# Plain products for the first 1024 columns of each MLP, and the seven products' activation sums made beside them

## The chip, the core and the metric

The kernel runs on one core of one Trainium2 chip. The metric is the device time of one execution in microseconds (us). TensorE (PE in the profile) multiplies; VectorE (DVE) and ScalarE (ACT) prepare its operands and clear its accumulators; SyncE (SP) issues the loads of the weights; GpSimd (POOL) issues the adding transfers of the residual stream.

## What is computed

Two decoder layers on 256 tokens of width 2048, each with an attention part and an MLP. The part that matters here is the MLP, twice:

```python
def sq_relu_mlp(h, w_up, w_down):
    u = jax.nn.relu(h @ w_up)
    return (u * u) @ w_down
...
        h = h + sq_relu_mlp(rmsnorm(h, mlp_norm[i]), w_up[i], w_down[i])
```

`w_up` is 2048 x 8192 and `w_down` 8192 x 2048, all in float32. The gain of the norm is put into the activations before the product, and the scale of each row of tokens, which comes out of the squared activations as its square, is applied when the output of `w_down` is added to the residual stream.

## The kernel before

**Numbers.** A float32 number is carried as a high part and a rest, both in the reduced form that TensorE takes (`fp32r`). `split` (L191 to L194) makes both: ACT copies to the high part (L193), DVE subtracts it from the source (L194). A product of two such numbers is three matmuls (`mm3`, L196 to L199: high with high, high with rest, rest with high). The three of a `gemm` stand in its line L410.

**Weights.** They arrive in tiles `wraw` of two chunks of 128 rows by 1024 columns (1 MB a load). Three such tiles lie in the pool `wp`. In an MLP (`more[0]` set) three more in the pool `mlp` are taken in turn with them, and two of those three first hold something else: `gx`, the activations of one half of the 2048 inputs, for as long as sums are still to be made from them. The split weights lie in `whi` (5 buffers in an MLP) and `wlo` (5), each 128 x 1024.

**An MLP.** The 8192 inner columns are taken in eight blocks of 1024 (`NE = 8`). `up(e)` makes block e of `h @ w_up`; `down(e - 1)` then multiplies the block before it with its rows of `w_down`, in two `gemm`s of 8 chunks by 12 matmuls. So the order is up 0, up 1, down 0, up 2, down 1, and so on. Between up 0 and up 1 stands nothing else.

**Seven products.** `up(e)` treats 12 of the 16 chunks of inputs in the way of Strassen (the Winograd form): for a pair of chunks, its partner four chunks on, two blocks of 128 tokens and two of 512 columns, seven products take the place of eight. `seven` is called three times a block, for chunks (0, 1), (8, 9) and (10, 11) with their partners. Each call has seven `product`s of 6 matmuls (L197 to L199), each with its own split of 128 x 1024 weights, and four differences of weights on DVE (L775, L777, L779, L782). The other four chunks (2, 3, 6, 7) are multiplied plainly by four calls of `plain`, 12 matmuls and one split each. Together that is 174 matmuls of 512 columns, 25 splits and 12 differences a block. The eight accumulators fill all of PSUM: six `acc` and the two `side` banks, which transposes use too.

**The activations for it.** `form_steps` transposes the residual stream on PE (L302), copies it with the gain to `gx` on ACT (L319) and splits seven forms of each half: a11, a12, a22 as they are, and s1, s2, s4, s3, which are sums made on DVE (L327). Those of half 0 are made beside the second `gemm` of `project` (the output projection of the attention part). Half 1 needs the columns that this `gemm` finishes: its transposes follow at once, and its seven forms (`late`) come within `up(0)`, where three plain calls stand first and `seven` of half 0 next.

**Order.** Every engine runs its own list in a fixed order. The lists are made by a scheduler that takes instructions in the order of the code, but lets one that is ready by its own reckoning pass one that is not; a load is issued when a tile of its pool comes free. So work that stands late in the code can run early, and the order of loads is not that of the code.

After `up(0)` its block is squared and transposed at once (`flush`), ahead of `up(1)`: L821 and L822 on ACT, L421 on PE, L423 on ACT, L424 on DVE. For the other blocks that runs beside a `down`.

Of the kernel before, what the change touches and what calls it, by code (L numbers as in the profile page):

```python
# [11 lines left out]
F32 = mybir.dt.float32  # L12
# [80 lines left out]
def yoco_kernel(ctx: ExitStack, tc: tile.TileContext, x, a_w_in, a_w_out, w_kv, b_w_q, b_w_out, w_up, w_down,  # L93
# [199 lines left out]
    def form_steps(halves, half, which):  # L293

        n, plain, f = halves[half]

# [27 lines left out]
        def sum_form(name, a, b, op):  # L324
# [4 lines left out]

        on_pe = [lambda c=c: split_plain(c) for c in range(2)] if plain is not None else []  # L330
        on_pe += [lambda c=c, c2=c2: take(c, c2) for c in range(2) for c2 in range(n // 2)]
        add, sub = ALU.add, ALU.subtract
        rest = [lambda: split_form("a11", a11), lambda: split_form("a12", a12),
                lambda: sum_form("s1", a21, a22, add), lambda: sum_form("s2", a11, "s1", sub),
                lambda: sum_form("s4", a12, "s2", add), lambda: sum_form("s3", a11, a21, sub),
                lambda: split_form("a22", a22)]
        return on_pe, rest

# [53 lines left out]
    def gemm(stat, ks, w, row0, cols, evac, width=HALF, before=None, first_raw=None, by_column=False):  # L392
# [287 lines left out]
    def project(oTs, w, gain_next, cut, again):  # L680


        st = Stats()
        stat = stat_of(oTs)
        cols = [(n * GW, n * GW + HALF) for n in range(2)]
        forms = []

        def heads_done(k=cut):
            if k == cut:
                flush()  # L690
                open_scope("mlp")
# [9 lines left out]
        on_pe, rest = form_steps(forms, 0, gain_next)  # L701
        enqueue([(run(on_pe + rest), len(on_pe + rest))], 8)
        gemm(stat, range(cut if again else 0, KC), w, 0, cols[1], residual(st, 1), by_column=True)
        flush()
        on_pe, rest = form_steps(forms, 1, gain_next)
        for step in on_pe:
            step()
        return st, forms, rest

    st, xm, late = project(oTs, a_w_out[0], G_M0, CUT_A, True)  # L710


    NE = DFF // GW

    def mlp(i, xm, late, st_in, gains_next, final=None):


        us = {}
        more[0] = True
        r2 = st_in.inv_square()  # L720

        def up(e):

            if e == 0:

                q5, q7, q2, q4, q3, q8 = (ps.tile([P, HALF], F32, name="acc") for _ in range(6))
                q1, q6 = side(), side()
            else:  # L730
                q1, q6, q5, q7, q3, q8 = (ps.tile([P, HALF], F32, name="acc") for _ in range(6))
                q2, q4 = side(), side()
            banks = dict(q1=q1, q2=q2, q3=q3, q4=q4, q5=q5, q6=q6, q7=q7, q8=q8)
# [54 lines left out]
            def nearly_done():  # L788
                if e:
                    plain(1, 0)  # L790
                nc.scalar.copy(c11, q1)
# [3 lines left out]

            if e == 0:
                plain_rows()
                plain(0, 0)
                plain(0, 1)
                plain(1, 0)  # L800
# [5 lines left out]
            else:  # L806
# [6 lines left out]
            for c, q in ((c21, q4), (c12, q3), (c22, q8)):  # L813
                nc.vector.tensor_tensor(c, q, c, op=add)
            tiles = [new_xt() for _ in range(2)]
            us[2 * e], us[2 * e + 1] = tiles

            def transposes():
                yield
                for n, t, c in ((0, 0, c11), (0, 1, c21), (1, 0, c12), (1, 1, c22)):  # L820
                    nc.scalar.activation(c, c, AF.Relu)  # L821
                    nc.scalar.activation(c, c, AF.Square)  # L822
# [3 lines left out]

            enqueue([(transposes(), 6)], 6)
            if e == 0:
                flush()

        st = Stats()
# [13 lines left out]
        for e in range(NE):  # L845
            up(e)
            if e:
# [6 lines left out]

    st, (xkv, xq) = mlp(0, xm, late, st, [G_KV, G_B])
    open_scope("keep", "att")
# [81 lines left out]

    st, xm, late = project(oTs, b_w_out[0], G_M1, CUT_B, False)

# [80 lines left out]

    mlp(1, xm, late, st, [], final)
    scope[0].close()
# [34 lines left out]
```

## Time and profile before

| | |
|---|---|
| three runs | 2211.4, 2213.1 and 2213.3 us, median 2213.1 |
| the profiled execution | 2211.9 us, of which its span (first to last instruction) 2210.0 us |
| granted TensorE clock | 0.995 of full, mean of the span |
| DVE split `wlo` (L194), 128 x 1024 | 1.22 us, one every 1.14 us in a row |
| ACT high part `whi` (L193), 128 x 1024 | 1.05 us |
| DVE difference of weights (L775 and so on) | 1.22 us, one every 1.14 us in a row |
| load of 1 MB of `w_up` | 4.8 us at least from issue to landing, 6.4 median, 9.4 at most |

A time in a row of the profile is that of the engine itself: how long an instruction took, from when, and in brackets how long the engine sat idle before it and whose signal ended that. Matmuls overlap, so their own durations (0.39 us) are longer than the distance from one to the next. The chain of waits follows the work that ended last back from the end, step by step; a stretch of it reads in order of time.

### The profile page before, as it was taken

How to read it: one execution, taken by the hardware profiler on the slowest of the kernel's cores; microseconds unless marked ns; L12 is line 12 of the kernel's file. 1: busy time of each engine (PE TensorE's matmuls, PEld its weight loads, DVE VectorE, ACT ScalarE, POOL GpSimd, SP SyncE). 2: the span in 40 equal slices, each digit the busy share in tenths (PEclk: the TensorE clock that was granted, in tenths of full speed). 3: DMA queues.
4: the chain of work that ended last, by engine and by line, in shares of the span. 5: the costliest groups of instructions: out<-in, count | busy, mean ns of one | idle time of the engine just before them, and what ended most of it. 6: DMA issues, size and time to landing. Idle time of an engine off the chain costs nothing.

```text
span 2210.0 us, 27845 instructions
## 1 busy us (share of the span) xinstructions
PE 2163.2 (98%) x10310; PEld 1784.1 (81%) x10310; DVE 1687.7 (76%) x2259; ACT 1293.9 (59%) x1736; POOL 99.7 (5%) x118
## 2 busy tenths in 40 slices
PE   9999997999999999999999999997999999999998
PEld 7788885788888888888888888885788888888886
DVE  5877769977977977957577777659978978878864
ACT  6445565665756656656455555455756656666663
POOL 0000000010010010010000000000010010010100
PEclk9999999999999999999999999999999999999999
DMA  8454454677777667683554555564577676677682
GB/s 305 156 188 140 147 190 153 228 210 228 225 206 250 203 206 244 208 246 126 174 160 154 161 158 167 171 210 145 171 217 238 213 228 225 205 226 247 195 262 77
DMA packets 164105, 434.44 MB, mean 197 GB/s; under 512 B 12800, under 2 KB 62080, under 8 KB 163968
## 3 DMA queue, kind: packets, MB, share of 16 engines
q1 hardware_dynamic: 146688, 401.25, 53.5%
q0 software_dynamic: 16128, 29.37, 7.5%
q10 hardware_dynamic: 1152, 2.04, 0.3%
q8 instruction: 81, 1.33, 0.2%
q14 instruction: 56, 0.46, 0.1%
HBM read 401.15 MB, written 2.10 MB: 182 GB/s over the span
## 4 chain that ended last, share of the span: by engine, by line
PE 90%; DVE 6%; ACT 2%; DMA 1%; issue 1%; DVEq 0%; ACTq 0%
PE acc L410 59%; PE acc L198 6%; PE acc L197 5%; PE acc L199 5%; PE side L197 4%; PE side L199 3%; PE side L198 3%; DVE wlo L194 3%; PE side L421 2%; ACT whi L193 1%; DMA wraw<-in_w_down_dram 1%; DVE wraw L779 1%; DVE wraw L777 0%; DMA wraw<-in_w_up_dram 0%; DVE wraw L775 0%
## 5 line engine op out<-in xcount | busy, mean ns | idle before, releaser
L193 ACT CAST whi<-wraw 128x1024 fp32r<-128x1024 f32 (+2 forms) x925 | 928.8, 1020 | 779.4 <-PE acc L410 515.7
L194 DVE TENSOR_TENSOR wlo<-wraw,whi 128x1024 fp32r<-128x1024 f32 (+2 forms) x925 | 1074.7, 1181 | 380.9 <-ACT whi L193 246.1
L410 PE MATMUL acc<-whi,xt 128*128 128x512 f32 x4160 | 1110.7, 380 | 3.8 <-ACT b L669 2.9
L410 PEld LDWEIGHTS acc<-whi,xt 128*128 128x128 f32 x4160 | 738.3, 188 | 141.9 <-ACT b L669 3.8
L410 PE MATMUL acc<-wlo,xt 128*128 128x512 f32 (+1 forms) x2080 | 618.5, 378 | 1.3 <-DVE wlo L194 1.3
L410 PEld LDWEIGHTS acc<-wlo,xt 128*128 128x128 f32 x2080 | 372.3, 188 | 75.0 <-DVE wlo L194 1.9
L670 POOL DMA_DIRECT2D h<-b x112 | 99.0, 1237 | 2060.6 <-ACT b L669 2042.6
L197 PE MATMUL acc<-whi,xt 128*128 128x512 f32 x356 | 140.8, 398 | 13.2 <-ACT whi L193 13.2
L198 PE MATMUL acc<-wlo,xt 128*128 128x512 f32 x356 | 140.1, 394 | 1.0 <-DVE wlo L194 0.9
L199 PE MATMUL acc<-whi,xt 128*128 128x512 f32 x356 | 139.6, 392 | 0.0
L198 PE MATMUL side<-wlo,xt 128*128 128x512 f32 x292 | 114.9, 394 | 3.5 <-DVE wlo L194 3.3
L197 PE MATMUL acc<-whi,xf 128*128 128x512 f32 x276 | 110.0, 399 | 5.8 <-ACT whi L193 5.5
L199 PE MATMUL side<-whi,xt 128*128 128x512 f32 x292 | 114.7, 393 | 0.0
L197 PE MATMUL side<-whi,xt 128*128 128x512 f32 x292 | 111.9, 392 | 0.0
L198 PE MATMUL acc<-wlo,xf 128*128 128x512 f32 x276 | 109.4, 396 | 0.9 <-DVE wlo L194 0.9
L199 PE MATMUL acc<-whi,xf 128*128 128x512 f32 x276 | 107.8, 391 | 0.0
L197 PEld LDWEIGHTS acc<-whi,xt 128*128 128x128 f32 x356 | 67.1, 189 | 32.9 <-ACT whi L193 19.8
L421 PE MATMUL side<-ident,b 128*128 128x128 f32 x512 | 77.2, 273 | 5.4 <-ACT b L822 4.9
L198 PEld LDWEIGHTS acc<-wlo,xt 128*128 128x128 f32 x356 | 67.1, 188 | 15.8 <-DVE wlo L194 2.5
L421 PEld LDWEIGHTS side<-ident,b 128*128 128x128 f32 x512 | 62.3, 140 | 20.5 <-ACT b L822 6.9
L199 PEld LDWEIGHTS acc<-whi,xt 128*128 128x128 f32 x356 | 67.1, 189 | 13.7
L669 ACT ACTIVATE b<-acc,ri 128x512 f32<-128x512 f32 x112 | 70.9, 686 | 4.1
(201 smaller groups left out, 1723.1 us busy)
## 6 DMA issues: line engine op xcount, KB each, us to landing
wraw<-in_w_up_dram SPq DMA_DIRECT2D x128, 1024.0 KB, 6.4
wraw<-in_w_down_dram SPq DMA_DIRECT2D x128, 1024.0 KB, 6.5
wraw<-in_b_w_q_dram SPq DMA_DIRECT2D x192, 256.0 KB, 3.1
wraw<-in_a_w_in_dram SPq DMA_DIRECT2D x31, 1024.0 KB, 5.2
h<-b POOLq DMA_DIRECT2D x112, 256.0 KB, 7.8
wraw<-in_a_w_out_dram SPq DMA_DIRECT2D x16, 1024.0 KB, 5.4
wraw<-in_b_w_out_dram SPq DMA_DIRECT2D x16, 1024.0 KB, 5.5
wraw<-in_w_kv_dram SPq DMA_DIRECT2D x8, 1024.0 KB, 5.0
```

Of the source, the lines that this page charges most:

```text
L193: nc.scalar.copy(hi, src)
L194: nc.vector.tensor_tensor(lo, src, hi.bitcast(F32), op=ALU.subtract)
L197: nc.tensor.matmul(o, a_hi, b_hi, start=start, stop=False)
L198: nc.tensor.matmul(o, a_hi, b_lo, start=False, stop=False)
L199: nc.tensor.matmul(o, a_lo, b_hi, start=False, stop=stop)
L410: nc.tensor.matmul(acc[t][i][:, :c1 - c0], stat(k, a, t), b[:, c0:c1], start=first and a == 0 and b is hi, stop=last and a == 1)
L421: nc.tensor.transpose(pt[:, j * P:(j + 1) * P], sr, ident)
L669: nc.scalar.activation(part, acc, AF.Copy, scale=scale()[:, t:t + 1])
L670: nc.gpsimd.dma_start(hh, part, accum_op=ALU.add)
L779: nc.vector.tensor_tensor(b22, b11, b22, op=sub)
```

## The change

Block 0 of each MLP is no longer made by `seven` and `plain`. A new `up_plain` multiplies all 16 chunks in a `gemm` of the ordinary kind: 16 splits, no differences, 192 matmuls, four accumulators. The chunks go in the order 2, 3, 0, 1, 8 to 11, 6, 7, 4, 5, 12 to 15, so that those of the first columns of each half (c = 0) come first. The split activations that it reads are the ones the seven products need anyway (a11, a12, a22); for a21, which they use only in sums, it is split into the place that s1 takes afterwards. The sums s1, s2, s4, s3 of both halves (`late`, eight steps) are queued at the ninth chunk, over seven pumps. `project` hands on the steps of half 1 instead of running its transposes. `up(e)` without its case for e = 0, and `squares`, which squares and transposes a block, are otherwise as they were; ACT now reads block 0 straight from the accumulators.

```diff
-        for k2 in range(ks[0], ks[-1], 2):
+        for k2 in ks[::2]:
...
+        firsts = []
+        for c, names in ((0, (("a11", a11), ("s1", a21))), (1, (("a12", a12), ("a22", a22)))):
+            firsts.append([lambda c=c: split_plain(c)] if plain is not None else [])
+            firsts[c] += [lambda c=c, c2=c2: take(c, c2) for c2 in range(n // 2)]
+            firsts[c] += [lambda a=a: split_form(*a) for a in names]
...
+        late = [lambda: sum_form("s1", a21, a22, add), lambda: sum_form("s2", a11, "s1", sub),
+                lambda: sum_form("s4", a12, "s2", add), lambda: sum_form("s3", a11, a21, sub)]
+        return firsts, late
...
-            if e == 0:
-                plain_rows()
-                plain(0, 0)
-                plain(0, 1)
-                plain(1, 0)
-                todo = run(late)
-                seven(0, 0, lambda: next(todo), lambda: next(todo))
-                for _ in todo:
-                    pass
-                seven(1, 0)
-            else:
-                seven(0, 0, plain_rows, lambda: plain(0, 0))
-                seven(1, 0, lambda: plain(0, 1))
+            seven(0, 0, plain_rows, lambda: plain(0, 0))
+            seven(1, 0, lambda: plain(0, 1))
...
+        def up_plain():
+            order = [2, 3, 0, 1, 8, 9, 10, 11, 6, 7, 4, 5, 12, 13, 14, 15]
+            def stat(k, hl, t):
+                half, r, j = k // 8, k // 4 % 2, k % 4
+                n, plain, f = xm[half]
+                if j >= n:
+                    return f["p", r, t][:, j - n, hl]
+                return f[(("a11", "s1"), ("a12", "a22"))[r][t]][:, j, hl]
+            def before(k):
+                if k == order[8]:
+                    for step in steps[1]:
+                        step()
+                    enqueue([(run(late), len(late))], 7)
+            for step in steps[0]:
+                step()
+            parts = []
+            gemm(stat, order, w_up[i], 0, (0, HALF), lambda t, s, acc: parts.append((s, t, b2(), acc)), before=before)
+            flush()
+            squares(0, parts)
```

Where this puts the work is seen in the lists of the engines. DVE at the start of the first MLP, before: `wraw_2922` holds chunks 2 and 3, `wraw_2974` and `wraw_2976` the pairs of the first `seven`, `wraw_2875` is `gx` of half 1.

```order
L194 TENSOR_TENSOR wlo_2979<-wraw_2974,whi_2978 128x1024
L775 TENSOR_TENSOR wraw_2974<-wraw_2974 128x2x512
L194 TENSOR_TENSOR xt_2513<-wraw_2875,xt_2513 128x4x128
L327 TENSOR_TENSOR b2_3056<-wraw_2875 128x512
L194 TENSOR_TENSOR xt_2513<-wraw_2875,xt_2513 128x4x128
L777 TENSOR_TENSOR wraw_2974<-wraw_2976,wraw_2974 128x2x512
L194 TENSOR_TENSOR wlo_2990<-wraw_2976,whi_2989 128x1024
L194 TENSOR_TENSOR wlo_3001<-wraw_2976,whi_3000 128x1024
L194 TENSOR_TENSOR wlo_3012<-wraw_2974,whi_3011 128x1024
L779 TENSOR_TENSOR wraw_2976<-wraw_2974,wraw_2976 128x2x512
```

The same place now: `wraw_2958` holds chunks 8 and 9, `wraw_2992` chunks 10 and 11, `wraw_2861` is `gx` of half 1 and `wraw_2668` that of half 0 (lines are two or three further down in the changed file).

```order
L194 TENSOR_TENSOR wlo_2977<-wraw_2958,whi_2976 128x1024
L364 RECIPROCAL ri_2862<-rv_2863 128x2
L194 TENSOR_TENSOR xt_2513<-wraw_2861,xt_2513 128x4x128
L194 TENSOR_TENSOR xf_2515<-wraw_2861,xf_2515 128x4x128
L328 TENSOR_TENSOR b2_3062<-wraw_2668 128x256
L328 TENSOR_TENSOR b2_3066<-wraw_2668,b2_3062 128x256
L328 TENSOR_TENSOR b2_3086<-wraw_2668,b2_3066 128x256
L328 TENSOR_TENSOR b2_3108<-wraw_2668 128x256
L194 TENSOR_TENSOR wlo_2995<-wraw_2992,whi_2994 128x1024
L194 TENSOR_TENSOR xf_2511<-b2_3066,xf_2511 128x2x128
```

The differences of weights are gone; the sums of half 0 (L328), which stood in `project`, have moved here, ahead of the splits of chunk 10, although the code queues them at chunk 6.

The loads of SP at the start of the second MLP, before: `wraw_12983` is for chunks 2 and 3, `wraw_13135` and `wraw_13137` for the second `seven`, `wraw_13213` and `wraw_13215` for the third, `wraw_12985` for chunks 6 and 7, `wraw_13035` and `wraw_13037` for the first `seven`.

```order
L743 DMA wraw_12983<-in_w_up_dram 128x2x1024
L743 DMA wraw_13135<-in_w_up_dram 128x2x1024
L743 DMA wraw_13137<-in_w_up_dram 128x2x1024
L743 DMA wraw_13213<-in_w_up_dram 128x2x1024
L743 DMA wraw_12985<-in_w_up_dram 128x2x1024
L743 DMA wraw_13035<-in_w_up_dram 128x2x1024
L743 DMA wraw_13037<-in_w_up_dram 128x2x1024
L743 DMA wraw_13215<-in_w_up_dram 128x2x1024
```

And now: chunks 2, 6, 4, 12, 0, 8, 10 and 14, each with the one after it.

```order
L390 DMA wraw_12912<-in_w_up_dram 128x2x1024
L390 DMA wraw_13048<-in_w_up_dram 128x2x1024
L390 DMA wraw_13112<-in_w_up_dram 128x2x1024
L390 DMA wraw_13154<-in_w_up_dram 128x2x1024
L390 DMA wraw_12946<-in_w_up_dram 128x2x1024
L390 DMA wraw_12980<-in_w_up_dram 128x2x1024
L390 DMA wraw_13014<-in_w_up_dram 128x2x1024
L390 DMA wraw_13196<-in_w_up_dram 128x2x1024
```

Chunk 0, which PE takes third, is the fifth load. The sixth (chunks 8 and 9) waits until the last sum of half 0 is made on DVE, the seventh (10 and 11) until chunk 1 is split; before, the seventh waited for the last sum of half 1. In the first MLP the order now is chunks 2, 0, 8, 12, 10, 14, 6, 4; there the seventh waits for the last sum of half 0 and the eighth for the split of chunk 11.

ACT in the second MLP, now, the last rows ahead of the high part of chunk 0 (`side_13050` and `side_13057` hold the transposed columns c = 1 of half 1):

```order
L320 ACTIVATE wraw_12883<-side_12897,gT_90 128x256
L193 CAST xf_12505<-b2_13108 128x2x128
L193 CAST xt_12507<-wraw_12883 128x4x128
L193 CAST xf_12509<-wraw_12883 128x4x128
L193 CAST xt_12504<-b2_13130 128x2x128
L320 ACTIVATE wraw_12883<-side_13050,gT_90 128x256
L320 ACTIVATE wraw_12883<-side_13057,gT_90 128x256
L193 CAST whi_12948<-wraw_12946 128x1024
```

Steps of both halves' activations now stand ahead of the weights of chunk 0 on ACT, two of them of columns that the code asks for only at the ninth chunk.

More of the change, by code (lines that the diff above doesn't have):

```diff
@@ L700, in project, with mlp @@
             gemm(stat, range(KC), w, 0, cols[0], residual(st, 0), before=heads_done, by_column=True)
-        on_pe, rest = form_steps(forms, 0, gain_next)
-        enqueue([(run(on_pe + rest), len(on_pe + rest))], 8)
+        firsts, late = form_steps(forms, 0, gain_next)
+        steps = firsts[0] + firsts[1]
+        enqueue([(run(steps), len(steps))], 8)
         gemm(stat, range(cut if again else 0, KC), w, 0, cols[1], residual(st, 1), by_column=True)
         flush()
[L705 to L710, printed above, removed]
+        steps, more_late = form_steps(forms, 1, gain_next)
+        return st, forms, steps, late + more_late
+    st, *xm = project(oTs, a_w_out[0], G_M0, CUT_A, True)
     NE = DFF // GW
-    def mlp(i, xm, late, st_in, gains_next, final=None):
+    def mlp(i, forms, st_in, gains_next, final=None):
+        xm, steps, late = forms
         us = {}
@@ L722, in up @@
         def up(e):
-            if e == 0:
-                q5, q7, q2, q4, q3, q8 = (ps.tile([P, HALF], F32, name="acc") for _ in range(6))
-                q1, q6 = side(), side()
-            else:
-                q1, q6, q5, q7, q3, q8 = (ps.tile([P, HALF], F32, name="acc") for _ in range(6))
-                q2, q4 = side(), side()
+            q1, q6, q5, q7, q3, q8 = (ps.tile([P, HALF], F32, name="acc") for _ in range(6))
+            q2, q4 = side(), side()
             banks = dict(q1=q1, q2=q2, q3=q3, q4=q4, q5=q5, q6=q6, q7=q7, q8=q8)
@@ L788, in nearly_done @@
             def nearly_done():
-                if e:
-                    plain(1, 0)
+                plain(1, 0)
                 nc.scalar.copy(c11, q1)
@@ L814, in up, with squares, work @@
                 nc.vector.tensor_tensor(c, q, c, op=add)
+            squares(e, [(0, 0, c11, c11), (0, 1, c21, c21), (1, 0, c12, c12), (1, 1, c22, c22)])
+        def squares(e, parts):
             tiles = [new_xt() for _ in range(2)]
             us[2 * e], us[2 * e + 1] = tiles
-            def transposes():
+            def work():
                 yield
-                for n, t, c in ((0, 0, c11), (0, 1, c21), (1, 0, c12), (1, 1, c22)):
-                    nc.scalar.activation(c, c, AF.Relu)
+                for n, t, c, src in parts:
+                    nc.scalar.activation(c, src, AF.Relu)
                     nc.scalar.activation(c, c, AF.Square)
@@ L825, in transposes @@
                                      [c[:, j * P:(j + 1) * P] for j in range(4)])
-            enqueue([(transposes(), 6)], 6)
+            enqueue([(work(), 6)], 6)
             if e == 0:
                 flush()
+        def up_plain():
[17 more added lines that the diff above has]
+            squares(0, parts)
         st = Stats()
@@ L845, in mlp @@
         for e in range(NE):
-            up(e)
+            if e:
+                up(e)
+            else:
+                up_plain()
             if e:
@@ L853, in mlp @@
         final(stat_of([us.pop(2 * NE - 2), us.pop(2 * NE - 1)]), w_down[i], (NE - 1) * GW, r2)
[L855 removed]
+    st, (xkv, xq) = mlp(0, xm, st, [G_KV, G_B])
     open_scope("keep", "att")
@@ L937, in yoco_kernel @@
             enqueue([(attend_b(kvh, t, qb[t], oTs[-1][:, pr * PAIR:(pr + 1) * PAIR]), steps_b(t)) for t in range(NT)], SPREAD_B)
-    st, xm, late = project(oTs, b_w_out[0], G_M1, CUT_B, False)
+    st, *xm = project(oTs, b_w_out[0], G_M1, CUT_B, False)
     def final(ustat, w, row0, r2):
@@ L1020, in final @@
         finish(1)
-    mlp(1, xm, late, st, [], final)
+    mlp(1, xm, st, [], final)
     scope[0].close()
```

10 lines of the change are left out of this document (removed).

## The prediction

> **What bounds the kernel now.** I read the page first, then the chain of waits in order of time, then busy times by stage.
>
> ```profile
> span 2210.0 us, 27845 instructions
> PE 2163.2 (98%) x10310; PEld 1784.1 (81%) x10310; DVE 1687.7 (76%) x2259; ACT 1293.9 (59%) x1736; POOL 99.7 (5%) x118
> PE 90%; DVE 6%; ACT 2%; DMA 1%; issue 1%; DVEq 0%; ACTq 0%
> ```
>
> PE carries 90% of the chain, so over the whole kernel matmuls cost their full price, and 10% of the chain is other work that PE waits for. The question is how much of that 10% lies in the changed stage. The chain, in order of time:
>
> ```profile
> 442.41 27.25 PE acc L410 x120
> ...
> 509.39 8.16 PE acc L410 x36
> ...
> 527.59 27.25 PE acc L410 x120
> ...
> 1596.32 8.17 PE acc L410 x36
> ```
>
> A `down` starts with the row of 36 matmuls, and its row of 120 comes 18.20 us later (527.59 - 509.39). The first row gives that of `down(0)` at 442.41, so in even running `down(0)` would have started at 424.21; in the second MLP it started at 1596.32. The row of 120 gives the pitch of a matmul, 27.25 / 120 = 0.2271 us. Block 0 starts here (the third column is the engine, x the count):
>
> ```profile
> 318.52 0.48 PE L197 MATMUL acc<-whi,xt 128*128 128x512 f32 x1
> ...
> 1484.43 0.48 PE L197 MATMUL acc<-whi,xt 128*128 128x512 f32 x1
> ```
>
> So from the start of up 0 to the start of `down(0)`, both blocks included, the first MLP takes 424.21 - 318.52 = 105.69 us and the second 1596.32 - 1484.43 = 111.89. What should two blocks take? An undisturbed one is next:
>
> ```profile
> 469.66 0.23 PE acc L197
> ...
> 517.55 0.44 PE side L421 x4
> ```
>
> From 469.66 to 509.39 are 39.73 us (174 x 0.2271 = 39.5: no waiting at all). Four transposes in a row take 0.44. In each of the two stretches lie two blocks and 32 transposes (16 of half 1, 16 of the squared block): 2 x 39.73 + 8 x 0.44 = 82.98 us. PE therefore loses 105.69 - 82.98 = 22.71 us in the first MLP and 28.91 in the second, **51.6 us** in all. What it waits for:
>
> ```profile
> 318.50:424.20 105.70, 92.73 (x389) 68.37 (x387) 102.66 (x109) 67.94 (x88) 0.00 (x0) 0.98 0.54 184
> 1484.40:1596.30 111.90, 93.57 (x382) 69.68 (x381) 102.27 (x107) 69.79 (x89) 0.00 (x0) 0.94 0.47 162
> 469.20:554.40 85.20, 85.20 (x384) 70.16 (x383) 68.98 (x66) 53.97 (x63) 7.07 (x9) 1.00 0.71 222
> ```
>
> Columns: stretch, length, busy PE, PEld, DVE, ACT, POOL, granted clock, DMA share, GB/s. In both stretches DVE is busy for over 102 us: 97% of the first. In an even period of one block and one `down` (third row) it is busy for 69 of 85. Two blocks of seven products behind each other ask DVE for 2 x (25 splits + 12 differences), with the half 1 forms between, and no `down` in which to work ahead. The chain between 345 and 426 says the same of the waits:
>
> ```profile
> by line: DVE wlo L194 33.3%; issue 12.8%; DVE wraw L779 7.2%; DVE wraw L777 7.2%; DMA wraw<-in_w_up_dram 6.0%; DVE wraw L775 5.7%; ACT whi L193 4.7%; DVE wraw L782 2.8%; ACT b L821 2.7%; DVE xt L424 2.4%; PE acc L197 2.1%; PE acc L199 2.0%;
> ```
>
> Splits and differences of weights together hold 56% of that chain, loads 6%. So this stage is bound by DVE.
>
> The page's idle column would give a smaller loss: PE not busy for 105.70 - 92.73 = 13.0 and 111.90 - 93.57 = 18.3 us, and a change that removed only this would come to 2196 after the terms below. The Trainium skill, in Perfetto Trace Analysis, section Identifying the Most-Contended Engine, holds matmul busy time to be a poor measure because matmuls are pipelined. The trace agrees: 82.98 us of work read as 92.73 busy. I go by the pitch.
>
> **The change part by part.** *Matmuls.* 192 instead of 174 in block 0: 18 x 0.2271 = 4.09 us (39.73 becomes 43.60, +3.87 against the block as measured), with nothing to hide it on PE: **+7.7** for both MLPs.
>
> *DVE in block 0.* 25 splits and 12 differences become 16 splits. From the chain:
>
> ```profile
> 332.26 1.14 DVE wraw L779
> ...
> 389.14 3.49 DVE wlo L194 x3
> ```
>
> A difference costs 1.14, a split in a row 1.14 to 1.16: 21 x 1.14 = 24 us of DVE go, as much as PE lost in a stretch. What stays for it in the plain block is 16 splits (18.2), four splits of half 1 (2.4), the sums and splits of half 1 (4.8) and half 0 (2.7), and 2.9 of additions to the residual: 31 us beside 43.6 of matmuls. So DVE is late nowhere by its load. Since five buffers of `whi` and `wlo` let it go five chunks ahead, it paces itself by PE and has 12 us left over for block 1. I take the wait for DVE within the plain block as **0**.
>
> *Does each operand come in time?* Durations first (mean ns behind the comma): the statistics, a copy to `gx`, a square, a rest of 512 columns, and the landing of the loads of `w_up`.
>
> ```profile
> L352 ACT ACTIVATE b<-h 128x512 f32<-128x512 f32 (+1 forms) x41 | 25.2, 615 | 32.5 <-DVE h L675 18.6 <-DVE h L673 9.5 <-DVE h L1017 4.4
> L319 ACT ACTIVATE wraw<-side,gT 128x256 f32<-128x256 f32 x24 | 10.6, 468 | 1.6 <-PE side L302 1.6
> L822 ACT ACTIVATE b<-b 128x512 f32<-128x512 f32 x64 | 38.8, 625 | 0.6
> L424 DVE TENSOR_TENSOR xt<-side,xt 128x512 fp32r<-128x512 f32 x64 | 43.7, 683 | 0.9 <-ACT xt L423 0.9
> ...
> DMA to landing us min/median/max: 4.8/6.4/9.4
> ```
>
> In a row each of these takes some 0.1 less, as their ends overlap. The last additions to the residual before end so:
>
> ```profile
> 319.32 1.28 DVE L673 TENSOR_TENSOR h<-acc,h 128x512 f32<-128x512 f32 x2
> ```
>
> at 320.6. In the first MLP a11 and a21 of half 1 follow that, a statistic or two, four copies with one split of weights between them on ACT (1.2 + 1.8 + 1.0) and two splits of both parts (1.8): 327, with PE at chunk 8 from 318.5 + 4 x 2.73 + 0.9 for eight transposes = 330.3. The four sums of half 0 stand next on DVE; the seventh load (chunk 6) starts behind them at 328.5, and with 6.4 us and a split (1.04 + 1.14) its chunk is ready by 337; PE wants it at 341. The eighth (chunk 4) starts at the split of chunk 11, some 3 us later, and is wanted at 347. No wait: **0**. In the second MLP the loads stand worse.
>
> ```profile
> 1479.86 1.39 SPq L743 DMA_DIRECT2D wraw<-in_w_up_dram  x3
> ...
> 1486.97 0.16 DVE L356 TENSOR_REDUCE rv<-ss 128x2 f32<-128x8 f32 x1 [1.42 <-ACT b L352]
> ...
> DMA to landing us min/median/max: 5.0/5.1/9.4
> ```
>
> The first row is the fourth to sixth load before, the last the landing of loads from 1465 to 1520. Chunk 0, now the fifth load, can start at 1480.3, where the fifth started before, and is there by 1489.7 at the latest. But ACT comes to it only after the statistics (1486.9), six copies, two splits of 512 and three of 256 columns (4.5 us), two of the copies not before PE has finished chunk 3 (1484.43 + 2 x 2.73 + 8 x 0.11 = 1490.8); its high part is ready at 1492.9. PE, with the 16 transposes done early, is there at 1491.7: a wait of 1.2, and 0.2 for the low part. Chunk 8's load starts behind the last sum of half 0 at 1488.1 (the reduction above stands between the sums, and waits for ACT), lands at 1493.2, and is split by 1497.1; PE wants it at 1498.6. Chunk 10's starts at the split of chunk 1, 1495.3, and is split by 1502.6, wanted at 1504. I take **1.4**, between 0 and the one wait of this kind in the trace:
>
> ```profile
> 1499.55 0.68 DVE L327 TENSOR_TENSOR b<-wraw 128x512 f32<-128x512 f32 x1
> ...
> 1500.62 4.96 DMA wraw<-in_w_up_dram
> ...
> 1506.69 0.79 PE L197 MATMUL acc<-whi,xt 128*128 128x512 f32 x1 [5.37 <-ACT whi L193]
> ```
>
> The sum that ends at 1500.2 gave free the tile of the seventh load, which started at once (second row, from the chain), and PE sat 5.37.
>
> *The end of block 0.* PE has to wait for the squares of the last accumulators, as before; ACT reads them a step earlier, without DVE's additions. The waits of this kind before are one group:
>
> ```profile
> PE side L421 <- ACT b L822: 4.9, 3, 2.8
> ```
>
> 4.9 us, three times, in the two blocks 0; I keep **2.4** each. At most it doubles; at least it is nothing, as up 1's first matmuls stand between the transposes.
>
> *Block 1.* 39.73 us if DVE starts as far ahead as in even running. By its list it has, at the end of block 0, done four of the 25 splits and four of the 12 differences: 9.1 us within the 12 left over. Behind that, ACT serves four Relu, four squares and four copies, about 0.6 each, among the next high parts, which holds DVE's queue for some 5 us. What DVE has to do from there to the last split is 21 x 1.14 + 8 x 1.14 + 5 x 0.6 = 36.1, and with 5 lost and 2.5 of matmuls behind the last split 43.6, against PE's own 39.73 + 1.77 of transposes + 2.4. Even, so I add **0.7**; the bounds are 0 and 4.8 (the first rival).
>
> *Else.* The same bytes are loaded. `project` loses DVE work beside a `gemm` in which PE does not wait: 0. Away from these stages the lists differ in few places.
>
> **Sum.** Each stretch: 43.60 + 39.73 + 3.52 of transposes + 2.4 + 0.7 = 89.95 us, in the second MLP 1.4 more. 105.69 - 89.95 = 15.7 and 111.89 - 91.35 = 20.5: **36.3 us less** than the profiled execution's 2211.9, 2175.6. The median of the runs is 1.2 above that execution, so I say **2176**.
>
> **Rivals.** *DVE without its lead.* If ACT's squares or late raw tiles cost DVE its 9 us, block 1 runs at DVE's rate: 37 x 1.14 + 12 x 0.6 (eight additions and four parts of the squares) = 49.4 instead of the 44.6 above: +4.8 each, **2185**. For it: in even running DVE works from 471.7 to the end of the block almost without a gap, so little is spare. Against: the first split of block 1 needs only a buffer.
>
> *Late loads.* Two waits of 5.37 in each MLP where a load hangs on a sum or on the split before it: 4 x 5.37 less the 1.4 counted, +20, **2196**. For it the rows above; against it the margins of 1.5 us in the second MLP and over 4 in the first. The Trainium skill, in TensorE: Matmul & The Clock Gate, section What's actually happening, says that an idle window of about 3.4 us halves the clock until one such window of work is done; by that each of these waits would cost an estimated 1.7 us more, 2203. The trace agrees as far as it goes: the two stretches were granted 0.98 and 0.94, the even one 1.00.
>
> *The other side: matmuls for nothing.* If the 51.6 us are not DVE's work but what a block without a `down` before it costs (tiles held by `gx`, loads one by one), they stay, and only the 7.7 us of matmuls are new: **2220**. It decides from 44 us of waiting on, 22 in each MLP, about 8 loads of 5.4 in a chain. Against: loads hold 6% of the chain, splits and differences 56%.
>
> *The change doesn't do what it says* if the sums stand ahead of the splits; on DVE those of half 0 do, which is in the sum above at 1.35 us and nothing waits; with the forms of half 1 ahead too it would be the late-load case.
>
> **How the numbers follow.** About 0.2% (4.4 us) is what a measurement of this kernel can tell from no change. The forecast and its neighbours (all waits gone, 2211.9 - 51.6 + 7.7 = 2168, up to 2181) have 0.70; DVE without lead 0.15; late loads 0.09; matmuls for nothing 0.03; a balance near nothing 0.03. The range **2167 to 2191** takes in the first two and the milder half of late loads. Faster 0.94, same 0.03, slower 0.03.
>
> **What would show it.** Plain block: 192 matmuls of line L412 within 47 us from its first, no idle over 1.5 us before them; DVE near 70% busy there. End of block 0: waits before the transposes of 2 to 3 us a block. Block 1: under 45 us; if DVE is over 97% busy in it and PE idles before L197, the lead is gone. `down(0)` near 408.5 and, counted from its own up 0, 91 us after it in the second MLP. Wrong would be waits over 5 us for `whi` behind a load, or block 1 as slow as before.

## The result, and the profile after

| | before | changed |
|---|---|---|
| runs | 2211.4 to 2213.9 us, median 2213.2 | 2177.6, 2179.0, 2179.4, 2179.8 us, median 2179.2 |
| the profiled execution, and its span | 2211.9, 2210.0 us | 2177.6, 2175.8 us |
| PE lost in the two stretches (below) | 22.5 and 28.9 us | 4.3 and 4.5 us |

The changed kernel takes 0.9846 of the time before (95% interval 0.9829 to 0.9864), 34.0 us less; 36.3 were forecast. The page, busy times and chain by engine:

```profile
span 2175.8 us, 27830 instructions
PE 2156.5 (99%) x10346; PEld 1789.2 (82%) x10346; DVE 1634.4 (75%) x2205; ACT 1276.8 (59%) x1720; POOL 99.7 (5%) x118
PE 93%; DVE 3%; ACT 2%; DMA 1%; issue 1%; SPq 0%; DVEq 0%; ACTq 0%
```

PE holds 93% of the chain instead of 90%, with 36 matmuls more (x10346). Where the plain block starts, from PE's rows in order of time (start, length, engine, line, count), in the first and the second MLP:

```profile
319.06 0.71 PE L412 MATMUL acc<-whi,xt 128*128 128x512 f32 x2
...
1470.47 0.71 PE L412 MATMUL acc<-whi,xt 128*128 128x512 f32 x2
```

And the rows of 120 matmuls of `down(0)`, with an undisturbed pair behind them, from the chain:

```profile
428.37 27.23 PE acc L412 x120
495.37 8.16 PE acc L412 x36
513.59 27.23 PE acc L412 x120
...
1579.99 27.25 PE acc L412 x120
```

A `down` in even running starts 513.59 - 495.37 = 18.22 us ahead of its row of 120. So the first stretch is 428.37 - 18.22 - 319.06 = 91.1 us (before 105.7, forecast 89.95), the second 1579.99 - 18.22 - 1470.47 = 91.3 (before 111.9, forecast 91.35). They gave 14.6 and 20.6 us. Up 0 itself starts 0.54 later in the first MLP, which `project` lost. Busy times by stage (stretch, length, PE, PEld, DVE, ACT, POOL, granted clock, DMA share, GB/s):

```profile
319.00:410.10 91.10, 89.43 (x407) 72.29 (x405) 79.33 (x91) 59.90 (x84) 0.00 (x0) 1.00 0.63 218
1470.40:1561.80 91.40, 89.92 (x407) 72.31 (x405) 78.50 (x89) 62.86 (x87) 0.00 (x0) 1.00 0.59 202
319.00:364.60 45.60, 45.60 (x209) 37.43 (x208) 36.85 (x48) 29.09 (x47) 0.00 (x0) 1.00 0.71 254
368.80:406.70 37.90, 37.20 (x164) 29.73 (x163) 37.38 (x36) 25.00 (x28) 0.00 (x0) 1.00 0.59 188
```

DVE is busy for 79 of 91 us instead of 103 of 106, and the granted clock is 1.00 in both stretches (0.98 and 0.94 before). In the plain block (third row) it has 45.60 - 36.85 = 8.8 us free, and PE is busy all the time. In block 1 (fourth row) it is busy for 37.38 of 37.90 us: the slack is gone there. What PE waits for, first MLP and second (us, times, longest):

```profile
PE side L423 <- ACT b L811: 2.1, 1, 2.1
PE acc L197 <- ACT whi L193: 0.6, 1, 0.6
```

```profile
PE acc L412 <- DVE wlo L194: 1.1, 1, 1.1
PE acc L197 <- ACT whi L193: 0.5, 1, 0.5
PE acc L412 <- ACT whi L193: 0.5, 1, 0.5
PE side L303 <- ACT wraw L320: 0.3, 1, 0.3
```

The largest, L423, is new and was not in the forecast. The chain behind it:

```profile
399.10 3.50 DVE wlo L194 x3
402.61 5.95 DMA wraw<-in_w_down_dram
408.60 0.04 issue
408.64 1.05 ACT whi L193
409.69 0.53 ACT b L810
410.22 0.47 ACT xt L425
410.69 0.54 ACT b L811
411.23 0.04 issue
411.27 0.33 PE side L423
```

DVE's splits free a raw tile at 402.6, and only then a load of `w_down` can start. ACT stands at that load's high part until 408.6, with the squares of block 1 queued behind it, and PE waits for their transposes. It is DVE without its lead, one step further on than block 1.

### The profile page after: what moved, and what is told of

Same layout as the page of the kernel before. It is cut to its first block, busy times and chain, and to the rows that moved or that the text cites. A ratio compares the mean times of both kernels' runs of the same rounds, so it can differ in the third digit from the quotient of the medians.

```text
span 2175.8 us, 27830 instructions
## 1 busy us (share of the span) xinstructions
PE 2156.5 (99%) x10346; PEld 1789.2 (82%) x10346; DVE 1634.4 (75%) x2205; ACT 1276.8 (59%) x1720; POOL 99.7 (5%) x118
## 4 chain that ended last, share of the span: by engine, by line
PE 93%; DVE 3%; ACT 2%; DMA 1%; issue 1%; SPq 0%; DVEq 0%; ACTq 0%
PE acc L412 64%; PE acc L198 5%; PE acc L199 5%; PE acc L197 5%; PE side L197 3%; PE side L199 3%; PE side L198 3%; PE side L423 2%; DVE wlo L194 2%; DMA wraw<-in_w_down_dram 1%; ACT whi L193 1%; PE side L303 0%; PE side L908 0%; DVE b L554 0%; DMA b<-in_xt_dram 0%
## 5 line engine op out<-in xcount | busy, mean ns | idle before, releaser
L193 ACT CAST whi<-wraw 128x1024 fp32r<-128x1024 f32 (+2 forms) x907 | 912.5, 1020 | 771.9 <-PE acc L412 541.5
L194 DVE TENSOR_TENSOR wlo<-wraw,whi 128x1024 fp32r<-128x1024 f32 (+2 forms) x907 | 1054.4, 1182 | 404.1 <-ACT whi L193 270.6
L412 PE MATMUL acc<-whi,xt 128*128 128x512 f32 (+1 forms) x4368 | 1170.3, 381 | 3.8 <-ACT b L671 3.1
L412 PEld LDWEIGHTS acc<-whi,xt 128*128 128x128 f32 x4368 | 776.4, 188 | 150.4 <-ACT b L671 3.9
L412 PE MATMUL acc<-wlo,xt 128*128 128x512 f32 (+1 forms) x2184 | 651.4, 379 | 1.3 <-DVE wlo L194 1.3
L198 PE MATMUL acc<-wlo,xt 128*128 128x512 f32 x288 | 112.2, 390 | 0.0
L197 PE MATMUL acc<-whi,xt 128*128 128x512 f32 x288 | 112.0, 390 | 0.1
L199 PE MATMUL acc<-whi,xt 128*128 128x512 f32 x288 | 112.0, 389 | 0.0
L199 PE MATMUL side<-whi,xt 128*128 128x512 f32 x280 | 109.1, 390 | 0.0
L197 PE MATMUL side<-whi,xt 128*128 128x512 f32 x280 | 106.7, 389 | 0.0
L198 PE MATMUL acc<-wlo,xf 128*128 128x512 f32 x252 | 99.6, 395 | 0.0
L197 PE MATMUL acc<-whi,xf 128*128 128x512 f32 x252 | 98.3, 390 | 1.1 <-ACT whi L193 1.1
L199 PE MATMUL acc<-whi,xf 128*128 128x512 f32 x252 | 98.4, 391 | 0.0
L423 PE MATMUL side<-ident,b 128*128 128x128 f32 x512 | 76.9, 273 | 2.5 <-ACT b L811 2.1
L423 PEld LDWEIGHTS side<-ident,b 128*128 128x128 f32 x512 | 62.0, 140 | 17.6 <-ACT b L811 3.6
L197 PEld LDWEIGHTS acc<-whi,xt 128*128 128x128 f32 x288 | 53.9, 188 | 12.0 <-ACT whi L193 0.9
L199 PEld LDWEIGHTS acc<-whi,xt 128*128 128x128 f32 x288 | 54.1, 188 | 11.1
```

The lines of the kernel that those rows point to most:

```text
L193: nc.scalar.copy(hi, src)
L194: nc.vector.tensor_tensor(lo, src, hi.bitcast(F32), op=ALU.subtract)
L197: nc.tensor.matmul(o, a_hi, b_hi, start=start, stop=False)
L198: nc.tensor.matmul(o, a_hi, b_lo, start=False, stop=False)
L199: nc.tensor.matmul(o, a_lo, b_hi, start=False, stop=stop)
L412: nc.tensor.matmul(acc[t][i][:, :c1 - c0], stat(k, a, t), b[:, c0:c1], start=first and a == 0 and b is hi, stop=last and a == 1)
```

## The experiments

Each kernel was timed in turn with the kernel before, and differences are taken against the median of before in the same comparison (2212.7 to 2213.7 us). An interval is about 0.0015 of the ratio to either side, some 3 us. "Lost" is what PE lost in the two stretches: in the profiled execution, from up 0's first matmul to the rows of `down(0)`, the distance from each PE start to the next less 0.227 us for 512 columns or 0.11 for a transpose, summed. This counts waits and slow matmuls alike, and is good to some 0.5 us.

| kernel | median us | ratio to before (95%) | against before | lost, first and second MLP |
|---|---|---|---|---|
| before | 2213.2 | 1 | 0 | 22.5, 28.9 |
| changed | 2179.2 | 0.9846 (0.9829 to 0.9864) | -34.0 | 4.3, 4.5 |
| before_no_diff | 2194.6 | 0.9914 (0.9899 to 0.9929) | -18.2 | 15.7, 18.4 |
| before_no_sums | 2202.5 | 0.9954 (0.9939 to 0.9969) | -10.2 | 20.4, 22.2 |
| before_no_diff_sums | 2183.0 | 0.9864 (0.9849 to 0.9878) | -29.7 | 9.9, 13.9 |
| before_16_splits | 2175.8 | 0.9831 (0.9814 to 0.9847) | -36.9 | 6.4, 9.4 |
| after_dve8 | 2179.6 | 0.9849 (0.9834 to 0.9863) | -33.3 | 7.8, 5.5 |
| after_dve16 | 2195.0 | 0.9917 (0.9901 to 0.9934) | -17.9 | 13.4, 11.4 |
| after_sums_late | 2209.3 | 0.9979 (0.9970 to 0.9989) | -3.6 | 11.6, 27.8 |
| after_plain4 | 2186.4 | 0.9880 (0.9864 to 0.9897) | -26.3 | 4.4, 4.9 |
| after_no_diff1 | 2170.9 | 0.9808 (0.9793 to 0.9823) | -41.8 | 0.6, 2.2 |
| after_pool1 | 2181.3 | 0.9853 (0.9838 to 0.9867) | -32.4 | 6.0, 7.3 |
| after_pool2 | 2183.4 | 0.9863 (0.9849 to 0.9878) | -30.3 | 7.0, 8.7 |
| after_halves | 2181.8 | 0.9851 (0.9835 to 0.9868) | -31.9 | 7.6, 5.2 |

### Were the waits before DVE's work?

Four kernels take work off DVE in the stretches of the kernel before and leave the 174 matmuls of block 0. First the differences:

```diff
                 product(b11, (f["a11"], "q1"))
-                nc.vector.tensor_tensor(b11, b12, b11, op=sub)
+                if e:
+                    nc.vector.tensor_tensor(b11, b12, b11, op=sub)
...
```

> The kernel before, with the 12 differences of weights of block 0 left out in both MLPs (the products take the blocks as they were loaded, so the output is not the reference's); splits, loads, matmuls and their order of use are kept. Theory DVE (the 51.6 us of waiting in the two stretches are DVE's work): 12 x 1.14 = 13.7 us less on DVE in each stretch, which comes out of PE's waits: stretches of 92 to 95 and 98 to 101 us, 22 to 27 us less in all, 2186 to 2191. Rival structure (a block without a down before it waits for its loads and for the tiles that gx holds, whatever DVE does): the waits stay, 0 to 5 us less, 2208 to 2213.

18.2 us went, less than the 22 to 27 of the DVE theory and far more than the 0 to 5 that the rival allows. Nothing but DVE's instructions is missing here, so the differences are a cause, and not the only one. Then the sums:

```diff
     rest = [lambda: split_form("a11", a11), lambda: split_form("a12", a12),
-            lambda: sum_form("s1", a21, a22, add), lambda: sum_form("s2", a11, "s1", sub),
-            lambda: sum_form("s4", a12, "s2", add), lambda: sum_form("s3", a11, a21, sub),
             lambda: split_form("a22", a22)]
...
-                product(b11, (f["s1"], "q5"))
+                product(b11, (f["a12"], "q5"))
...
```

> The kernel before without the sums s1, s2, s4, s3 of both halves in both MLPs (the products take a11, a12 and a22 in their places, so the output is not the reference's); all differences, splits of weights, loads and matmuls are kept. In each stretch 4 sums and 4 splits of 512 columns, 8 x 0.6 = 4.8 us, leave DVE, the products no longer wait for them, and the tile of gx comes free for a load earlier. Theory DVE (only its amount of work counts): 4.8 us a stretch, 10 in all, 2203 (2200 to 2207). Rival place (the sums stand in front of the weights on DVE and hold the loads): what is left of the waits without the differences, 15.7 - 4.3 and 18.4 - 4.4, goes with the sums instead: 15 to 25 in all, 2188 to 2198.

10.2 us, DVE's 2 x 4.8 us to within the measurement; the rival, with 15 to 25, falls. Both at once:

> The kernel before without the differences of block 0 and without all sums of activations (both parts as in the two runs that leave out one; the output is not the reference's). Theory DVE: 18.2 us as measured without the differences and 10 to 15 for the sums, 2180 to 2185. With the place of the sums as a cause of its own all waits that the change removed go: about 34 + 7.7 (there are no added matmuls), 2171 to 2176. Rival structure (loads one by one and the squares at the end of block 0 hold PE without either): 2188 to 2195.

29.7 us, where the two apart make 28.4: within the uncertainty they add, as work on one engine would. That is in the DVE theory's 2180 to 2185. Still 9.9 and 13.9 us were lost. The last kernel of the four cuts the splits as well, by letting one split block serve two products:

```diff
+                if e == 0:
+                    product(b11, (f["a11"], "q1"), (f["a12"], "q5"))
+                    within()
+                    product(b12, (f["a22"], "q7"))
+                    product(b22, (f["a11"], "q3"), (f["a11"], "q6"))
+                    before_last()
+                    product(b21, (f["a12"], "q2"), (f["a22"], "q4"))
+                    return
```

> The kernel before with DVE's list for the weights of block 0 cut to that of the plain block: no differences, no sums of activations (as in before_no_diff_sums), and 16 splits instead of 25, since each split block serves two products at once where it did before in two splits; 174 matmuls, eight accumulators and their additions, the loads and the squares behind them stay (the output is not the reference's). Theory DVE (what is left beside the 29.7 us is the 9 splits, 9 x 1.14 = 10.3 us a stretch): 12 us less than before_no_diff_sums at least, the changed kernel without its added matmuls, 2179.2 - 7.7 = 2171.5, down to 2165. Rival structure (the waits that before_no_diff_sums still has, 9.9 and 13.9 us in the two stretches, are the squares at the end of block 0, some 5.8 and 4.5 us with the slow matmuls behind them, and the loads at the start of the second MLP, 6 us, which the plain block avoids by its four accumulators and its order of chunks): these 16 us stay, 5 to 8 us less, 2175 to 2178.

7.2 us more: the DVE theory's 12 at least were missed, and the rival's 5 to 8 came, but for half of its reason only. PE's waits for squares (us in total, times, longest) in before_no_diff_sums and in before_16_splits:

```profile
PE side L419 <- ACT b L824: 4.0, 3, 1.5
```

```profile
PE side L419 <- ACT b L828: 2.1, 1, 2.1
```

The three waits of the first row stand at the ends of the blocks 0. They went with the splits, so they were not what a block's end costs by itself; the one left stands at the start of `down(0)`, as in the changed kernel. What did stay is the start of the second MLP. The chain of before_16_splits there, and PE's rows behind it:

```profile
1474.42 0.94 ACT wraw L319 x2
1475.37 0.02 issue
1475.39 1.14 ACT xt L193 x2
1476.53 0.95 ACT whi L193
```

```profile
1477.53 0.73 PE L197 MATMUL acc<-whi,xt 128*128 128x512 f32 x2 [1.29 <-ACT whi L193]
1478.79 0.50 PE L198 MATMUL acc<-wlo,xt 128*128 128x512 f32 x1 [0.53 <-DVE wlo L194]
```

The rival had late loads here, and the chain has none: ACT copies and splits half 1 ahead of the first weights. So 36.9 us came back without a plain product. Not all of it is shown to be DVE's alone: with every sum and every split of weights that is left out, ACT's copy to the high part goes too (9 copies of 1.05 us in each block 0), and no run here takes these off ACT by themselves. For DVE speaks that it was busy for 97% of the first stretch and ACT for 67.94 of 105.70 us, and that the differences, which are DVE's only, gave half of the 36.9. The changed kernel removed 34.0 + 7.7 (its added matmuls) = 41.7, which is 4.8 more. At the start of the second MLP it loses some 2 us less than before_16_splits; the rest of the 4.8 was not isolated.

### How much slack has DVE in the plain block?

Work is added to it: a maximum of the loaded weights with themselves, behind every second split or behind each.

```diff
                     split(hi[:, c0:c1], lo[:, c0:c1], raw[:, k - k2, c0:c1])
+                    if more_dve[0] and k % 2:
+                        nc.vector.tensor_tensor(raw[:, k - k2, c0:c1], raw[:, k - k2, c0:c1], raw[:, k - k2, c0:c1], op=ALU.max)
```

> The changed kernel with 8 added DVE instructions in each plain block, one behind every second split (a maximum of the loaded weights with themselves, in place, 128x1024, 1.14 us each in a row; values unchanged): 9.1 us of DVE a block. In the plain block of the first MLP DVE has gaps of 8.5 us in all. Theory DVE with slack in the plain block: hidden but for 0 to 2 us a block, 2179 to 2183. Rival DVE is the bound in the plain block too: 9 us each, 2197. Rival structure: 2179, as the theory; only the next run tells these apart.

> As the run with 8, but one behind each of the 16 splits, 18.2 us of DVE a block. Theory DVE with slack: 18.2 less the 8.5 of gaps = 9.7 us a block, found as PE waits late in the plain block or as block 1 without its lead; 19 us in all (14 to 26), 2198 (2193 to 2205). Rival DVE is the bound already: 18 each, 2215. Rival structure (DVE does not set the time here): 0 to 4 us, 2179 to 2183.

Against the changed kernel 8 instructions a block cost 0.7 us in all, 16 cost 16.1. 18.2 us of work in two plain blocks are all but free, and 36.4 cost 16.1 (19 expected): the free part is about 10 us a block. So DVE is neither the bound in the plain block (2197 and 2215) nor without effect (2179 to 2183 with 16). The trace agrees for 16: 24.8 us lost instead of 8.8. With 8, 13.3 were lost in the profiled execution, which at 2182.0 was the slowest of the four; about 1.5 of that is a clock granted at 0.50 from 414.4 to 417.7 us, behind the wait at the start of `down(0)`.

### The sums behind the plain block

One number of each `gx` is rewritten from the block's last accumulator, so that the sums cannot be made before it. This is a place where neither kernel has them: before, those of half 0 were made in `project` and those of half 1 in up 0.

```diff
-                    enqueue([(run(late), len(late))], 7)
...
+            for one in gx_ends[-2:]:
+                acc = parts[-1][3][:, :1]
+                nc.vector.scalar_tensor_tensor(one, acc, 0.0, one, op0=ALU.mult, op1=ALU.add)
+            for step in late:
+                step()
             squares(0, parts)
```

> The changed kernel with its second part undone: the sums s1, s2, s4, s3 of both halves can only be made behind the plain block (one number of each gx tile is rewritten, unchanged in value, from the block's last accumulator, so that all eight sums wait for it). Theory: 7.5 us of sums and splits leave the slack of the plain block and stand in block 1, in which DVE has no gap from 368.8 to 406.7; the first seven products wait for s1 to s3 besides, and two of the six raw tiles stay gx for the whole plain block, so the loads of block 1 come late. 8 to 13 us a block, 16 to 26 in all, 2195 to 2205. Rival (only the smaller number of splits and differences counts, the place of the sums does not): 0 to 4 us, 2179 to 2183.

30.4 us, more than expected: 2209.3, and all but 3.6 of the gain is gone. The second MLP pays most. PE's waits there:

```profile
PE side L426 <- ACT b L814: 7.0, 1, 7.0
PE acc L415 <- ACT whi L193: 5.1, 3, 2.5
PE side L197 <- DVE xt L429: 1.4, 1, 1.4
```

The 7.0 were in no theory. From the chain:

```profile
1533.44 0.23 DVE wraw L846 x2
...
1538.44 0.61 DVE b L330
...
1539.60 1.08 ACT b L813 x2
1540.68 0.51 ACT xt L193
1541.18 1.05 ACT b L814 x2
```

ACT has the high parts of the sums to make, in DVE's pace, and the squares of block 0 (L813, L814) stand behind them in its list; PE wants their transposes. The 5.1 are in the main the plain block's own loads, which found two of six raw tiles held as `gx`. Not all of the loss is waiting: behind waits of this kind the clock was granted at 0.50 for 23.9 us of the two stretches (13.7 of them from 1539.8 on), which made the matmuls there some 9 us longer; in the changed kernel it was 1.00 throughout. So the place of the sums can take back nearly the whole gain: plain products with the sums behind them bring next to nothing. What a plain block would bring with the sums of half 0 left in `project` was not run.

### What do the added matmuls cost?

Block 4, where PE does not wait, is made plain as well (`up_plain(e)`, without the steps for the activations):

```diff
-            if e:
-                up(e)
+            if e in (0, 4):
+                up_plain(e)
             else:
-                up_plain()
+                up(e)
```

> The changed kernel with block 4 of each MLP in plain products too, 192 matmuls in place of 174 (its a21 is read where s1 stands by then, so the output is not the reference's). There PE does not wait, so the 18 matmuls should cost their pitch, 18 x 0.227 = 4.1 us a block, 7.7 to 8.2 in all: 2187. Rival (the smaller load on DVE and the loads give something back at the blocks behind it): 0 to 5 us, 2179 to 2184.

7.7 us, the forecast's figure, within the 3 us of uncertainty; nothing that could be measured comes back in a place where DVE was not the limit.

### What is left, and can it be had?

The differences of weights of block 1 are left out of the changed kernel:

```diff
-                nc.vector.tensor_tensor(b11, b12, b11, op=sub)
+                if e != 1:
+                    nc.vector.tensor_tensor(b11, b12, b11, op=sub)
...
```

> The changed kernel with the 12 differences of weights of block 1 left out in both MLPs (the output is not the reference's). Theory (what is left of PE's waits in block 1 and at the start of down(0) is DVE without its lead): the waits of 0.3, 0.8 and 2.3 us in the first MLP and 0.7 and 1.3 in the second go, 5.3 us less, 2174. Rival (the wait at the start of down(0) is a load that comes late by itself): only the waits before L197 go, 1.8 us, 2177.5; the waits of 2.3 and 1.3 stay in the trace.

7.8 us less, where 5.3 were expected, and in the first MLP hardly anything is lost (0.6). The wait of 2.1 at the start of `down(0)` went with it, though nothing was changed on that load; so it comes from DVE's missing lead. Two kernels try to have this by giving differences of block 1 to GpSimd, one of each four and then two:

```diff
-                nc.vector.tensor_tensor(b21, b21, b22, op=add)
+                (nc.gpsimd if e == 1 else nc.vector).tensor_tensor(b21, b21, b22, op=add)
```

> The changed kernel with the last difference of each of the three calls of seven in block 1 of both MLPs made by GpSimd instead of DVE (3 of 12 a block). Without any of the 12, 8.2 us went. Theory (DVE's amount of work in block 1 is what is left to gain, and GpSimd works beside it): 3 x 1.14 = 3.4 us less on DVE a block against 3.7 us of waits, 5 to 7 us less, 2172 to 2174. Rival (GpSimd's own time, which no trace shows for such an operation, or its use of the same memory holds up the product that waits for it, or DVE): no gain or a loss, 2179 to 2190.

> As the run before with two differences of each call on GpSimd (6 of 12 a block). Theory: all waits of block 1 and of the start of down(0) go, 7 to 8 us less, 2171 to 2173. Rival: twice the loss of the run before where that loses; where one a call just fits, the second comes late (two products behind its split instead of at the end of its seven): 2178 to 2200.

Against the changed kernel they are 1.6 and 3.7 us slower, which is at the edge of what can be measured; the gain of 5 to 8 us that the theory had did not come. In the stretches more is lost than the changed kernel's 8.8 (13.3 and 15.7 us). GpSimd and DVE at one time, from after_pool1:

```profile
363.37 2.39 POOL L779 TENSOR_TENSOR wraw<-wraw 128x1024 f32<-128x1024 f32 x1 [362.06 <-DVE wraw L776]
```

```profile
363.45 3.39 DVE L194 TENSOR_TENSOR wlo<-wraw,whi 128x1024 fp32r<-128x1024 f32 x1 [0.23 <-ACT whi L193]
```

The split beside it took 3.39 us instead of 1.22: it ended 363.45 + 3.39 - (363.37 + 2.39) = 1.1 us behind GpSimd, so it ran when GpSimd was done. Here DVE paid 2.2 us to save 1.14. The last kernel changes the order of the chunks:

```diff
-            order = [2, 3, 0, 1, 8, 9, 10, 11, 6, 7, 4, 5, 12, 13, 14, 15]
+            order = [2, 3, 0, 1, 6, 7, 4, 5, 8, 9, 10, 11, 12, 13, 14, 15]
...
-                    for step in steps[1]:
+                    for step in steps[0] + steps[1]:
```

> The changed kernel with the plain block's chunks in the order 2, 3, 0, 1, 6, 7, 4, 5, 8 to 15: half 0 whole first, and all transposes, copies and splits of half 1 at its ninth chunk. Theory on the wait before chunk 0 in the second MLP (ACT has the statistics and copies of half 1 to do ahead of that chunk's high part): its 1.4 us go. Theory of the lead: the sums of half 1 come some 10 us later, still within the plain block, whose slack covers 9 us: 0 to 2 us a block lost. Together 2177 to 2182; the trace tells: no PE wait in the first 15 us of the plain block of the second MLP. Rival: the wait is chunk 0's load and stays.

2.1 us slower than the changed kernel, within the uncertainty. In its trace chunk 0's wait is gone from the second MLP, as the theory on it said, but the transposes of half 1 now stand in one piece and wait for their copies, so 5.2 us are lost there instead of 4.5. Of the 7.6 lost in the first MLP some 1.4 are a halved clock behind the wait at `down(0)` (last section). Of the three that do all the work in another way, none beats the changed kernel.

## Why the prediction was right, and what was off

**The bound.** 2176 was forecast and 2179.2 measured, for the reason given: DVE. By the pitch PE had lost 51.6 us; with DVE's work (and the ACT copies that go with it) taken away step by step, 36.9 came back without a plain product. The rival of matmuls for nothing (2220) is excluded by these runs. Its mechanism, tiles held by `gx`, is real: it shows where the sums are put late. Some 6 of the 51.6 us were not waits themselves but slow matmuls behind them: before, the clock was granted at 0.50 from 342.8 to 346.2, 1503.3 to 1510.1 and 1551.1 to 1557.9 us, and nowhere in the changed kernel's stretches. The forecast had them in its loss by the pitch and said nothing of them as a term. That the page's idle column is too small a measure held: a gain of idle time alone would have been 2196. The Trainium skill, Perfetto Trace Analysis, section Identifying the Most-Contended Engine, says that matmul busy time is not a good measure of how close one is to the roofline, because pipelined instructions look smaller in the trace. This trace agrees that the measure is poor, but here they look larger: 92.73 us busy for 82.98 us of work.

**Matmuls.** +7.7 forecast, 7.7 measured in block 4.

**The plain block.** No PE wait for DVE in the first MLP, as forecast. DVE was to be near 70% busy; it was 36.85 / 45.60 = 81%. The 70% left out the four splits and four differences of block 1 (9.1 us) that the paragraph on block 1 had DVE do ahead; on the other side, a part of the first splits and of the additions to the residual stood before the block began.

**Operands in time.** 0 and 1.4 us forecast. In the first MLP nothing, in the second the waits for the copies and for chunk 0 of 0.3 and 0.5, some 1.4 us lost with the short waits right behind them. Late loads (2196) did not come.

**The end of block 0**, 2.4 us a block, was over-sized: nothing. PE's rows there:

```profile
364.65 0.39 PE L197 MATMUL acc<-whi,xt 128*128 128x512 f32 x1
364.92 1.18 PE L423 MATMUL side<-ident,b 128*128 128x128 f32 x8
365.85 0.48 PE L198 MATMUL acc<-wlo,xt 128*128 128x512 f32 x1
...
367.56 0.60 PE L423 MATMUL side<-ident,b 128*128 128x128 f32 x4
```

No row has a bracket with an idle time. ACT reads the accumulators without DVE's additions ahead of it, and the first products of up 1 stand between the transposes: the lower bound given was the right value.

**Block 1**, 0.7 us, was under-sized. The waits before L197 and at the start of `down(0)` make 3.3 us in the first MLP and 2.0 in the second (as lost time; the rows above have 0.6 + 2.1 and 0.5 + 1.1 of idle time). The balance "43.6 against ... even" ended at the last split of block 1. It left out who waits behind that split: the raw tile that it frees, a load of 5.95 us, ACT standing at it with the squares behind. So here the mechanism of the rival without the lead came in part, which the forecast had priced at 4.8 us a block.

**Sum.** 4.8 us over-sized at the end of block 0 and 5.3 - 1.4 = 3.9 under-sized in block 1 nearly cancel; that the total came so close is luck to this extent. Some 1 us a stretch, in steps of about 0.1 at changes between matmuls and transposes, had no term (4.3 lost, less the 3.3, in the first). So 35.2 came in the stretches (14.6 + 20.6) instead of 36.3; `project` lost 0.5 in the first MLP, where 0 was said, another 0.5 went outside the stretches and was not traced, and 34.2 are left between the spans of the profiled executions. What the forecast did not price at all is the place of the sums: beside the block no PE wait in the first MLP is theirs, behind it they cost 30.4.

## To carry to other kernels

Where an engine falls behind in one stage and has slack in the next, trading its work for matmuls pays only as far as its waits reach: price the matmuls at their pitch (distance from one start to the next), and check it by doing the same where nobody waits (7.7 us for nothing). Work that is taken off the path needs a place with slack; the same eight sums fitted into DVE's slack beside the block and cost 30 us behind it, where tiles, loads, another engine's queue and at last the clock hung on them. When a balance between two engines comes out even, follow what the last instruction of the late one sets free (a tile, a load, a queue behind it): the wait turns up there.

## What the runs showed of the hardware

**Slow matmuls behind a wait are a matter of its place in time.** At the start of `down(0)` the changed kernel waits 2.15 us and after_halves 2.18. The rows behind it, of the changed kernel and of after_halves:

```profile
411.27 0.33 PE L423 MATMUL side<-ident,b 128*128 128x128 f32 x1 [2.15 <-ACT b L811]
411.36 0.71 PE L412 MATMUL acc<-wlo,xt 128*128 128x512 f32 x2
411.91 0.63 PE L412 MATMUL acc<-whi,xt 128*128 128x512 f32 x2
412.38 0.62 PE L412 MATMUL acc<-wlo,xt 128*128 128x512 f32 x2
```

```profile
412.83 0.33 PE L423 MATMUL side<-ident,b 128*128 128x128 f32 x1 [2.18 <-ACT b L811]
...
413.63 1.05 PE L412 MATMUL acc<-whi,xt 128*128 128x512 f32 x2
414.49 1.05 PE L412 MATMUL acc<-wlo,xt 128*128 128x512 f32 x2
415.34 1.69 PE L412 MATMUL acc<-whi,xt 128*128 128x512 f32 x4
416.87 0.63 PE L412 MATMUL acc<-wlo,xt 128*128 128x512 f32 x2
```

In the first, two matmuls start every 0.47 us; in the second every 0.86, until 416.9, though the wait is the same. The Trainium skill, TensorE: Matmul & The Clock Gate, section What's actually happening, says that the clock is halved after an idle window of about 3.4 us, and that these windows run freely and do not start anew with the kernel. The trace agrees on the length: in after_halves the granted clock is 0.50 from 413.23 to 416.64 and 1.00 around it, and its changes in a run lie whole multiples of 3.413 us apart. It agrees on the phase: on that grid the wait of after_halves lies in one window, 409.82 to 413.23, with PE busy for 1.23 us of it, while that of the changed kernel falls on two, with 2.70 and 1.98 us busy, and its clock stays at 1.00. It doesn't agree that the window has to be idle: in all runs here, in and around the two stretches, every drop from 1.00 to 0.50 came behind a window in which PE was busy for 1.8 us or less of the 3.41, which is about half. Six windows with 1.4 to 1.8 us busy were not followed by a drop, so near half busy time alone does not decide it.

**GpSimd took DVE's time.** A `tensor_tensor` of 128x1024 within SBUF took 2.39 us at least on GpSimd (5.52 at most), against 1.22 on DVE, and a split that met it was held until it ended. Where DVE was first it was the other way round: at 383.4 in after_pool1 three splits took their usual 3.49 us, and GpSimd's instruction beside them took the 5.52. The Trainium skill, SBUF — State Buffer, section SBUF: two separate sides, says that the two share a pair of ports which one instruction holds to its end. The rows of after_pool1 agree: 3.39 us instead of 1.22.
